# Two-layer encoder, MLP with Strassen block products: four instead of six up chunks ahead, runs of four steps, and shared sums that ScalarE copies out and fills in again

## The chip, the core and the metric

One core of one Trainium2 chip runs the whole network in one launch. The metric is device microseconds, the median of several executions. TensorE is called PE here, VectorE DVE, ScalarE ACT, GpSimd POOL, and SyncE, whose queue issues most loads, SP. PSUM is the memory into which PE's matmuls add; SBUF is the core's other memory.

## The reference

The input is 256 tokens of width 2048. Each of two layers does attention and then a dense MLP:

```python
h = h + jnp.concatenate([mix, cross], axis=-1) @ w_o[i]
n = rms_norm(h, mlp_norm[i])
h = h + jnp.square(jax.nn.relu(n @ w_up[i])) @ w_down[i]
...
return rms_norm(h, final_norm)
```

`w_up` is 2048 x 8192 and `w_down` 8192 x 2048, in float32. The change touches only the MLP: the up product, the squared ReLU, and the down product with its sum into `h`.

## The kernel before

**Precision.** Every float32 operand is split into a high and a low part (`split`, L507 on ACT for the high one, L508 on DVE for the low one), and each product is three matmuls: high by high, high by low, low by high.

**Up chunks.** The 8192 columns of the up product are 64 chunks of 128. A chunk (`up_grains`) loads a megabyte of `w_up` (`raw_U`), splits it in two halves (`uh` on ACT, `ul` on DVE), and runs 48 matmuls 256 wide into `ps_u` (`products`, L411). `squared` then applies ReLU and square on ACT (L1113, L1114). Two chunks make a pair; after the second, DVE forms three more combinations of their four 128 x 128 blocks (`c`, L1122 to L1124), and the seven operands are split into `a_s` (high on ACT, low on DVE). The first `LEAD` = 6 chunks of a layer run by themselves.

**Steps.** The down product is done by Strassen's scheme for 2 x 2 blocks: the 256 tokens are two halves, a pair gives two blocks of the inner dimension, and the 2048 output columns are two halves q, each with two 512-wide blocks. One step (`down_grains`) is one pair and one half q. It loads four 512-wide blocks of `w_down` (`b`), forms combinations of them (`t`: one on ACT, L1165, with an add by a POOL DMA, L1166, and three on DVE, L1172 to L1174), splits them (`bh`, `bl`, and `th`, `tl`), and multiplies seven operand pairs into seven PSUM sums p1 to p7, 512 wide. The products p3, p1, p2 come first (9 matmuls, from `bh`, `bl`), then p7, p6, p4, p5 (12, from `th`, `tl`), each three matmuls at L1194, L1196 and L1197. Between the two groups PE runs one more up chunk, so that 58 steps carry the remaining 58 chunks: the order written out in `add_mlp` is first products, chunk's first half, chunk's second half, second products.

**Runs.** Steps with the same q follow each other in runs (`RUNS`): the seven sums stay in PSUM through a run and leave it at its end (`taken`). p2, p3, p4 belong to one output block each and are added into `h` by DVE (L1237). p1, p5, p6, p7 are shared by several output blocks: the first run of a half q copies them to `z` in SBUF by ACT (L1250), and each later run of that q adds to `z` by DVE (L1248). After the last run of a half, `folded` makes the four output blocks out of `z` by eight DVE instructions (four at L1261, four at L1237), queued with a gap of 3 grains of the plan, 0.5 at the very end.

**Plain chunks.** The inner dimension that the steps leave over (30 pairs are done for one half q, 28 for the other, of 32) is done plainly behind the steps (`plain_grains`), block after block of 512 output columns in the order `REST` = 2, 0, 1, 3: 1 + 1 + 2 + 2 chunks of 24 matmuls 512 wide, with operands `h_p`, `l_p` and `a_p`, into `ps_m` (L388, L391, L392). In layer 0 the finished blocks go into `h` (L1237), are squared for the next norm (L920, ACT), transposed (L626, DVE) and scaled into `nT` (L537 ACT, L538 DVE), the operand of layer 1's first projection, whose weights are split as `uh`/`ul` and `hi`/`lo`. In layer 1 the last block is cut into three pieces, the first token half 512 wide and the second in two of 256, and each is finished by `finish` (add L1405, squares L1415, scaling L1429 to L1431, output DMAs).

**What sets the order.** Each engine runs its instructions in the order of a plan that is written out in grains; loads, splits and copies are placed a set number of grains ahead of their use, `later(k, f)` puts `f` k grains on, and `past(f, x)` behind an instruction x. Each engine's queue is in order: an instruction that waits holds up those behind it.

Of the kernel before, what the change touches and what calls it, by code (L numbers as in the profile page):

```python
# [13 lines left out]
AF = mybir.ActivationFunctionType  # L14
# [21 lines left out]
FIRST_CHUNKS = 3  # L36
UPS = DFF // P

LEAD = 6

RUNS = ((1, 4), (0, 8), (1, 8), (0, 8), (1, 8), (0, 8), (1, 8), (0, 6))

STEPPED = [sum(n for x, n in RUNS if x == q) for q in range(2)]

# [115 lines left out]
def encoder_kernel(ctx: ExitStack, tc: tile.TileContext, t: dict, out: bass.AP):  # L160
# [206 lines left out]
    def later(n, fn, *args):  # L367
        pending.append((state["tick"] + n, fn, args))
# [778 lines left out]
    def down_grains(layer, n, begins, ends, sooner):  # L1147

        q, j = STEPS[n]
        own = {}  # L1150

        def load():
            own["b"] = at.side.tile([P, 4, 512], F32, tag="b", bufs=3, name="b")
            nc.sync.dma_start(own["b"].rearrange("p a b -> p (a b)"),
                              t[f"w_pair{layer}"][j * 2 + q])

        def behind(fn, far=4):

            return (lambda: past(fn, box["splits"][-far])) if n < 2 else fn

        def lift():

            b, s = own["b"], at.side.tile([P, 4, 512], F32, tag="T", bufs=2, name="t")
            own["t"] = s
            nc.scalar.activation(s[:, 3, :], b[:, 3, :], AF.Copy)  # L1165
            nc.gpsimd.dma_start(s[:, 3, :], b[:, 1, :], accum_op=ALU.add)  # L1166

        def pre():

            b, s = own["b"], own["t"]  # L1170
            with tc.issue_after(box["made"].ins) if n == 2 else nullcontext():
                nc.vector.tensor_tensor(s[:, 0, :], b[:, 3, :], b[:, 0, :], op=ALU.add)  # L1172
# [12 lines left out]
        def run(which, products):  # L1185
            if n == 0 and which == "first":
                open_strassen(layer)
            hi, lo = own.pop(which)
            a = box["a", j]
            for name, ai, bi in products:  # L1190
                if begins:
                    sum_of(name)
                ps, s = box["ps"][name], slice(bi * 512, (bi + 1) * 512)
                ins = nc.tensor.matmul(ps, a[:, 0, ai, :], hi[:, s], start=begins, stop=False)  # L1194
                pin(ins)
                nc.tensor.matmul(ps, a[:, 0, ai, :], lo[:, s], start=False, stop=False)  # L1196
                nc.tensor.matmul(ps, a[:, 1, ai, :], hi[:, s], start=False, stop=ends)  # L1197

        def after(products):
            if ends:  # L1200
                for name, _, _ in products:
                    taken(q, name)

        def after_second():
            after(SECOND)
            if ends:
                box["z_set"].add(q)
            if ends and j == STEPPED[q] - 1:
                folded(q, 0.5 if n == len(STEPS) - 1 else 3)

        return [Grain(lambda: run("first", FIRST), lambda: after(FIRST), load, behind(pre), behind(prep_first, 4 if n else 1),
                      (12, 8, 4) if sooner else (12, 5, 4), behind(lift)),
                Grain(lambda: run("second", SECOND), after_second, None, None, behind(prep_second), SOONER)]

    def open_strassen(layer):
# [23 lines left out]
    def taken(q, name):  # L1239

        ps, inv = box["ps"][name], box["inv"]
        if name in DIRECT:
            i, b = DIRECT[name]
            add_scaled(columns_of(i, q, b), ps, inv[:, i : i + 1])
            return
        z = box["z"][q][:, SHARED.index(name), :]
        if q in box["z_set"]:
            nc.vector.tensor_tensor(z, ps, z, op=ALU.add)  # L1248
        else:
            nc.scalar.activation(z, ps, AF.Copy)  # L1250

    DIRECT = {"p2": (1, 0), "p3": (1, 1), "p4": (0, 0)}
    SHARED = ("p1", "p5", "p6", "p7")
# [1 line left out]
    def folded(q, gap):  # L1255

        z1, z5, z6, z7 = (box["z"][q][:, n, :] for n in range(4))
        inv, ninv = box["inv"], box["ninv"]

        def add(d, x, y, op=ALU.add):  # L1260
            return lambda: nc.vector.tensor_tensor(d, x, y, op=op)  # L1261
# [4 lines left out]
        for n, fn in enumerate((out(1, 0, z1, inv), add(z6, z6, z1, ALU.subtract), add(z7, z6, z7, ALU.subtract),  # L1266
                                add(z6, z6, z5, ALU.subtract), out(1, 1, z6, inv), out(0, 0, z7, inv),
                                add(z7, z7, z5, ALU.subtract),
                                out(0, 1, z7, ninv))):
            later(1 + int(gap * n), lambda fn=fn: past(fn, box["splits"][-2]))  # L1270

    def plain_grains(layer, nb, at_chunk):
# [14 lines left out]
                box["rest"] = split(*own[c, hf], own[c][:, hf * HALF : (hf + 1) * HALF])  # L1287


        PIECES = [(c, hf, (2 - nc_ + c) * 4 + hf * 2, 2) for c in range(nc_) for hf in range(2)]  # L1290

        def begin():
            if nb == REST[0]:
# [58 lines left out]
    def down_done(layer, nb):  # L1352
        def f(w):
# [22 lines left out]
            if n < 2:  # L1376
                later(1, turn)
                later(3, come)
            elif n == 2:

                later(2, lambda: past(turn, box["rest"]))
                later(7, lambda: past(come, box["early", 1]))
# [394 lines left out]
```

## Time and profile before

| what | value |
|---|---|
| runs | 1992.29, 1992.8, 1993.76 us; median 1992.8 us |
| span of the profiled execution | 1991.2 us |
| PE busy | 1982.2 us, 100% of the span |
| DVE busy | 1717.2 us, 86% |
| ACT busy | 1330.5 us, 67% |
| POOL busy | 132.8 us, 7% |
| DMA, mean over the span | 225 GB/s |

The profiled execution is known by its span, from its first instruction to its last. Its time as a run isn't listed apart; the median of the runs is 1.6 us above the span, which is what lies around it. In rows of the timeline, the first number is the start in us, the second the duration, and the bracket at the end gives the idle time before and what ended it. In rows of groups, `xN` is the count, then follow busy us in all, mean ns of one, and the idle time before with what ended it. In rows of windows, the columns are the stretch, its length, then busy us of PE, PE's weight loads, DVE, ACT and POOL with their counts, the granted clock of PE, the DMA share and GB/s.

### The profile page before, as it was taken

The page shows a single profiled execution, that of the slowest core. Times are in us where ns is not written, and L with a number is a line of the kernel's source. Part 1 is how long each engine was busy: PE and PEld are TensorE (multiplying, and loading weights), DVE is VectorE, ACT ScalarE, POOL GpSimd, SP SyncE. Part 2 cuts the span into 40 slices and gives each one's busy share as a digit, 9 for nine tenths or more (in the row PEclk, how much of TensorE's full clock was granted, in tenths as well). Part 3 has the DMA queues.
Part 4 walks back from the last instruction along what each step waited for, and adds up shares of the span by engine and source line. Part 5 has one row for each costly group of instructions (what it writes and reads, how often), then busy time and mean ns, then how long its engine had stood idle before and what let it go on. Part 6 is the DMA issues. An engine that isn't in the chain of part 4 may idle for free.

```text
span 1991.2 us, 32845 instructions
## 1 busy us (share of the span) xinstructions
PE 1982.2 (100%) x12856; PEld 1800.9 (90%) x12856; DVE 1717.2 (86%) x2104; ACT 1330.5 (67%) x1861; POOL 132.8 (7%) x185
## 2 busy tenths in 40 slices
PE   9999999999999999999999999999999999999998
PEld 8999999899999999999998888889999999999997
DVE  6777767589899999999999879778998999999997
ACT  6655555577777777777676666667776777777674
POOL 0000000000000000000000011000000000000000
PEclk9999999999999999999999999999999999999999
DMA  7855555767777777777766765667777777777772
GB/s 291 321 194 203 208 187 184 271 194 246 234 229 233 227 225 238 238 236 227 219 217 211 246 216 174 220 194 249 237 224 235 226 227 237 233 238 228 225 237 104
DMA packets 107804, 447.21 MB, mean 225 GB/s; under 512 B 18561, under 2 KB 40321, under 8 KB 60289
## 3 DMA queue, kind: packets, MB, share of 16 engines
q1 hardware_dynamic: 90144, 413.38, 58.9%
q0 software_dynamic: 17216, 31.20, 9.7%
q8 instruction: 101, 1.65, 0.3%
q10 hardware_dynamic: 288, 0.52, 0.1%
q14 instruction: 55, 0.44, 0.1%
HBM read 397.78 MB, written 4.19 MB: 202 GB/s over the span
## 4 chain that ended last, share of the span: by engine, by line
PE 98%; ACT 1%; DVE 1%; issue 0%; DMA 0%; SPq 0%; DVEq 0%; POOL 0%; POOLq 0%; ACTq 0%
PE ps_u L411 35%; PE ps_s L411 9%; PE p L1194 9%; PE p L1197 9%; PE p L1196 9%; PE ps_m L391 8%; PE ps_m L392 8%; PE ps_m L388 8%; PE sc_ps L603 0%; PE sc_ps L605 0%; PE sc_ps L604 0%; PE av L696 0%; PE av L697 0%; PE av L698 0%; PE idle L240 0%
## 5 line engine op out<-in xcount | busy, mean ns | idle before, releaser
L411 PE MATMUL ps_u<-hT,uh 128*128 128x256 f32 x3812 | 663.4, 276 | 0.0
L411 PEld LDWEIGHTS ps_u<-hT,uh 128*128 128x128 f32 x3812 | 578.9, 188 | 5.5
L411 PE MATMUL ps_u<-hT,ul 128*128 128x256 f32 x1960 | 541.4, 276 | 0.0
L507 ACT ACTIVATE uh<-raw_U 128x1024 fp32r<-128x1024 f32 x262 | 276.8, 1057 | 201.5 <-PE ps_u L411 189.3
L411 PEld LDWEIGHTS ps_u<-hT,ul 128*128 128x128 f32 x1960 | 368.0, 188 | 0.0
L508 DVE TENSOR_TENSOR lo<-raw,hi 128x1024 fp32r<-128x1024 f32 (+1 forms) x215 | 255.0, 1190 | 107.8 <-ACT hi L507 106.8
L507 ACT ACTIVATE hi<-raw 128x1024 fp32r<-128x1024 f32 (+1 forms) x215 | 221.9, 1037 | 183.9 <-PE ps_m L392 93.4
L508 DVE TENSOR_TENSOR ul<-raw_U,uh 128x1024 fp32r<-128x1024 f32 x262 | 318.4, 1218 | 13.7 <-ACT uh L507 13.4
L508 DVE TENSOR_TENSOR tl<-t,th 128x2048 fp32r<-128x2048 f32 x116 | 265.5, 2289 | 70.3 <-ACT th L507 69.9
L507 ACT ACTIVATE th<-t 128x2048 fp32r<-128x2048 f32 x116 | 222.7, 1919 | 114.7 <-PE p L1197 114.7
L508 DVE TENSOR_TENSOR bl<-b,bh 128x1536 fp32r<-128x1536 f32 x116 | 203.1, 1751 | 0.0
L1194 PE MATMUL p<-th,a_s 128*128 128x512 f32 x464 | 181.2, 391 | 0.0
L1196 PE MATMUL p<-tl,a_s 128*128 128x512 f32 x464 | 181.0, 390 | 0.0
L1197 PE MATMUL p<-th,a_s 128*128 128x512 f32 x464 | 180.5, 389 | 0.0
L507 ACT ACTIVATE bh<-b 128x1536 fp32r<-128x1536 f32 x116 | 172.4, 1487 | 8.4
L1166 POOL DMA_DIRECT2D t<-b x116 | 100.7, 868 | 1143.5 <-ACT t L1165 1113.2
L411 PE MATMUL ps_s<-nT,hi 128*128 128x256 f32 x896 | 154.6, 277 | 0.0
L1197 PE MATMUL p<-bh,a_s 128*128 128x512 f32 x348 | 136.2, 391 | 0.0
L411 PEld LDWEIGHTS ps_s<-nT,hi 128*128 128x128 f32 x896 | 135.3, 188 | 0.2
L1196 PE MATMUL p<-bl,a_s 128*128 128x512 f32 x348 | 135.4, 389 | 0.0
L1194 PE MATMUL p<-bh,a_s 128*128 128x512 f32 x348 | 135.4, 389 | 0.0
L411 PE MATMUL ps_s<-nT,lo 128*128 128x256 f32 x448 | 124.2, 277 | 0.0
(308 smaller groups left out, 3573.0 us busy)
## 6 DMA issues: line engine op xcount, KB each, us to landing
raw_U<-in_w_up SPq DMA_DIRECT2D x128, 1024.0 KB, 5.7
b<-in_w_pair SPq DMA_DIRECT2D x116, 1024.0 KB, 5.8
raw<-in_w_o SPq DMA_DIRECT2D x32, 1024.0 KB, 4.9
t<-b POOLq DMA_DIRECT2D x116, 256.0 KB, 5.2
raw<-in_w_b SPq DMA_DIRECT2D x21, 1024.0 KB, 5.2
raw<-in_w_av SPq DMA_DIRECT2D x12, 1024.0 KB, 5.0
raw<-in_w_aq SPq DMA_DIRECT2D x12, 1024.0 KB, 4.9
raw<-in_w_ak SPq DMA_DIRECT2D x12, 1024.0 KB, 4.8
```

What stands on the lines that cost most here:

```text
L388: first = nc.tensor.matmul(ps, ah, hi[:, s], start=st, stop=False)
L391: nc.tensor.matmul(ps, ah, lo[:, s], start=False, stop=False)
L392: final = nc.tensor.matmul(ps, al, hi[:, s], start=False, stop=sp)
L411: ins = nc.tensor.matmul(ps, x, acts[:, k, part], start=k == n == 0, stop=k == KT - 1 and n == 2)
L507: first = nc.scalar.activation(dst_hi, src, AF.Copy)
L508: return first, nc.vector.tensor_tensor(dst_lo, src, dst_hi.bitcast(F32), op=ALU.subtract)
L1166: nc.gpsimd.dma_start(s[:, 3, :], b[:, 1, :], accum_op=ALU.add)
L1194: ins = nc.tensor.matmul(ps, a[:, 0, ai, :], hi[:, s], start=begins, stop=False)
L1196: nc.tensor.matmul(ps, a[:, 0, ai, :], lo[:, s], start=False, stop=False)
L1197: nc.tensor.matmul(ps, a[:, 1, ai, :], hi[:, s], start=False, stop=ends)
```

## The change

It sets `LEAD` to 4, so that a layer's steps start after four up chunks and there are 60 steps, 30 for each half q; one plain chunk is left for each of the four blocks, so a layer has 4 instead of 6. `RUNS` becomes sixteen runs: 2, then fourteen of 4, then 2. At the end of every run ACT copies the shared sums to `z`. At the start of the next run of that half, `seeded` has ACT copy `z` back into the PSUM sum, and the run's matmuls add to it; the DVE adds into `z` go. `folded` comes with a gap of 1 instead of 3 and makes one output block earlier; some loads are placed at other distances.

```diff
{DIFF}
```

Counted over the kernel: 84 more matmuls 512 wide in steps, 84 fewer 512 wide and 24 fewer 256 wide in plain chunks. ACT: 112 more copies `z<-p` (128 instead of 16) and 112 copies `p<-z`, four more each of `t`, `bh`, `th` and `u_0`, four fewer each of `h_p` and of the single left block `a_0`. DVE: the 48 adds `z<-p,z` go, the direct adds from p become 96 instead of 48, four more each of `bl`, `tl` and the three `t`, four fewer `l_p`. SP: two loads of `b` more and two plain loads fewer in a layer; POOL: four more DMA adds into `t`. Behind the change the lines of `taken` and later functions are numbered 4 to 6 higher (L1237 is L1241, L1261 is L1267, L1405 is L1411).

The first place is the start of layer 0's steps, on DVE. `tl` is the low part of the first step's second operands, `bl` that of the second step's first operands, `ul` a chunk's low half, `a_s` the low part of the second pair (chunks 2 and 3). Before:

```order
L1124 TENSOR_TENSOR c_4842<-c_4842 128x128
L508 TENSOR_TENSOR bl_4956<-b_4780,bh_4955 128x1536
L508 TENSOR_TENSOR ul_4989<-raw_U_4845,uh_4988 128x1024
L508 TENSOR_TENSOR a_s_4911<-c_4842,a_s_4911 128x896
L508 TENSOR_TENSOR ul_5029<-raw_U_4845,uh_5028 128x1024
L508 TENSOR_TENSOR tl_5070<-t_4811,th_5069 128x2048
```

The second pair's `a_s` stands ahead of the first `tl` (the last row). After the change:

```order
L508 TENSOR_TENSOR tl_4928<-t_4683,th_4927 128x2048
L1122 TENSOR_TENSOR c_4848<-c_4848 128x128
L508 TENSOR_TENSOR bl_4961<-b_4815,bh_4960 128x1536
L1123 TENSOR_TENSOR c_4848<-c_4848 128x256
L926 TENSOR_REDUCE ss_t_5023<-ssq0_130 128x2
L1124 TENSOR_TENSOR c_4848<-c_4848 128x128
L1172 TENSOR_TENSOR t_4957<-b_4922 128x512
L508 TENSOR_TENSOR ul_4991<-raw_U_4851,uh_4990 128x1024
L928 TENSOR_SCALAR full_5025<-ss_t_5023 128x2
L1173 TENSOR_TENSOR t_4957<-t_4957,b_4922 128x512
L508 TENSOR_TENSOR a_s_4919<-c_4848,a_s_4919 128x896
```

Now the first `tl` stands ahead, then `bl`, `ul` and the rest, and the second pair's `a_s` is the eleventh from it.

The second place is ACT where a run of q = 0 ends and one of q = 1 begins. `z0` and `z1` are the two halves' `z`, p7, p6, p5 the shared sums, `th` the high part of the next step's second operands, `c` the ReLU and square. After the change:

```order
L1113 ACTIVATE c_6321<-ps_u_6372 128x256
L1250 ACTIVATE z0_4652<-p7_6022 128x512
L1114 ACTIVATE c_6321<-c_6321 128x256
L1250 ACTIVATE z0_4652<-p6_6025 128x512
L1256 ACTIVATE p7_6454<-z1_4653 128x512
L1256 ACTIVATE p6_6457<-z1_4653 128x512
L1250 ACTIVATE z0_4652<-p5_6030 128x512
L507 ACTIVATE th_6469<-t_6257 128x2048
L1256 ACTIVATE p5_6462<-z1_4653 128x512
L507 ACTIVATE bh_6485<-b_6340 128x1536
```

Before, ACT had no fill anywhere, and `z` copies only at the end of each half's first run; at every other run's end DVE had:

```order
L1248 TENSOR_TENSOR z0_4652<-p7_7273,z0_4652 128x512
L508 TENSOR_TENSOR ul_8004<-raw_U_7859,uh_8003 128x1024
L1248 TENSOR_TENSOR z0_4652<-p6_7277,z0_4652 128x512
L1122 TENSOR_TENSOR c_7891<-c_7891 128x128
L1237 SCALAR_TENSOR_TENSOR first_83<-p4_7281,inv_5023,first_83 128x512
L1174 TENSOR_TENSOR t_7931<-t_7931,b_7910 128x512
L1248 TENSOR_TENSOR z0_4652<-p5_7285,z0_4652 128x512
L508 TENSOR_TENSOR tl_8029<-t_7827,th_8028 128x2048
```

The adds at L1248 have left DVE; ahead of ACT's `th` now stand three copies and two fills, and p5's fill stands behind it.

The third place is the boundary between the layers, on DVE. `ps_m` are sums of plain blocks, `n_t` and `n_z` the transposed blocks, `nT1` the operand of layer 1, `ul` and `lo` the lows of its weights. Before:

```order
L508 TENSOR_TENSOR ul_11416<-raw_U_11298,uh_11415 128x1024
L538 SCALAR_TENSOR_TENSOR nT1_11271<-n_z_11330,first_83,nT1_11271 128x256 x4
L508 TENSOR_TENSOR ul_11432<-raw_U_11298,uh_11431 128x1024
L1237 SCALAR_TENSOR_TENSOR first_83<-ps_m_11391,inv_5023,first_83 128x512
L1237 SCALAR_TENSOR_TENSOR first_83<-ps_m_11392,inv_5023,first_83 128x512
L508 TENSOR_TENSOR lo_11475<-raw_U_11355,hi_11474 128x1024
```

After:

```order
L1241 SCALAR_TENSOR_TENSOR first_83<-ps_m_11548,inv_5027,first_83 128x512
L538 SCALAR_TENSOR_TENSOR nT1_11474<-n_t_11478,first_83,nT1_11474 128x256 x2
L1241 SCALAR_TENSOR_TENSOR first_83<-ps_m_11549,inv_5027,first_83 128x512
L508 TENSOR_TENSOR ul_11565<-raw_U_11450,uh_11564 128x1024
L626 STREAM_TRANSPOSE n_t_11612<-first_83 128x4x4x32
L508 TENSOR_TENSOR ul_11595<-raw_U_11450,uh_11594 128x1024
L626 STREAM_TRANSPOSE n_t_11612<-first_83 128x4x4x32
L538 SCALAR_TENSOR_TENSOR nT1_11474<-n_z_11537,first_83,nT1_11474 128x256 x2
L1241 SCALAR_TENSOR_TENSOR first_83<-ps_m_11598,inv_5027,first_83 128x512
L538 SCALAR_TENSOR_TENSOR nT1_11474<-n_z_11537,first_83,nT1_11474 128x256 x2
L1241 SCALAR_TENSOR_TENSOR first_83<-ps_m_11599,inv_5027,first_83 128x512
L508 TENSOR_TENSOR lo_11648<-raw_U_11505,hi_11647 128x1024
```

Before, layer 1's first `ul` comes behind the transposes of the third block, and the last block's sums behind the second `ul`. After, the third block's sums (the first two L1241 here) stand between the `nT1` of the block before, right ahead of the first `ul`; the transposes of the third block stand around the second `ul`, and the last block's sums between the next four `nT1`, all of it ahead of the first `lo`.

More of the change, by code (lines that the diff above doesn't have):

```diff
@@ L37 @@
 UPS = DFF // P
-LEAD = 6
-RUNS = ((1, 4), (0, 8), (1, 8), (0, 8), (1, 8), (0, 8), (1, 8), (0, 6))
+LEAD = 4
+RUNS = ((1, 2), *((0, 4), (1, 4)) * 7, (0, 2))
 STEPPED = [sum(n for x, n in RUNS if x == q) for q in range(2)]
@@ L1190, in run @@
             for name, ai, bi in products:
-                if begins:
+                if n == 0:
                     sum_of(name)
+                entered = begins and not (name in SHARED and q in box["z_set"])
                 ps, s = box["ps"][name], slice(bi * 512, (bi + 1) * 512)
-                ins = nc.tensor.matmul(ps, a[:, 0, ai, :], hi[:, s], start=begins, stop=False)
+                ins = nc.tensor.matmul(ps, a[:, 0, ai, :], hi[:, s], start=entered, stop=False,
+                                       skip_group_check=True)
                 pin(ins)
-                nc.tensor.matmul(ps, a[:, 0, ai, :], lo[:, s], start=False, stop=False)
-                nc.tensor.matmul(ps, a[:, 1, ai, :], hi[:, s], start=False, stop=ends)
+                nc.tensor.matmul(ps, a[:, 0, ai, :], lo[:, s], start=False, stop=False, skip_group_check=True)
+                nc.tensor.matmul(ps, a[:, 1, ai, :], hi[:, s], start=False, stop=ends, skip_group_check=True)
         def after(products):
@@ L1202, in after @@
                     taken(q, name)
+                    if n + 1 < len(STEPS):
+                        seeded(STEPS[n + 1][0], name)
         def after_second():
@@ L1245, in taken, with seeded @@
             return
[L1246 to L1250, printed above, removed]
+        nc.scalar.activation(box["z"][q][:, SHARED.index(name), :], ps, AF.Copy)
+    def seeded(q, name):
+        ps = sum_of(name)
+        if name in SHARED and q in box["z_set"]:
+            nc.scalar.activation(ps, box["z"][q][:, SHARED.index(name), :], AF.Copy)
     DIRECT = {"p2": (1, 0), "p3": (1, 1), "p4": (0, 0)}
@@ L1266, in folded @@
         for n, fn in enumerate((out(1, 0, z1, inv), add(z6, z6, z1, ALU.subtract), add(z7, z6, z7, ALU.subtract),
-                                add(z6, z6, z5, ALU.subtract), out(1, 1, z6, inv), out(0, 0, z7, inv),
+                                out(0, 0, z7, inv), add(z6, z6, z5, ALU.subtract), out(1, 1, z6, inv),
                                 add(z7, z7, z5, ALU.subtract),
@@ L1381, in f @@
                 later(2, lambda: past(turn, box["rest"]))
-                later(7, lambda: past(come, box["early", 1]))
+                later(5, lambda: past(come, box["early", 1]))
             else:
```

6 lines of the change are left out of this document (3 added, 3 removed).

## The prediction

> **What bounds the kernel now.** I read the head of the page first, then the chain that ended last, then the waits of PE, then windows and timelines of single places.
>
> ```profile
> span 1991.2 us, 32845 instructions
> PE 1982.2 (100%) x12856; PEld 1800.9 (90%) x12856; DVE 1717.2 (86%) x2104; ACT 1330.5 (67%) x1861; POOL 132.8 (7%) x185
> PE 98%; ACT 1%; DVE 1%; issue 0%; DMA 0%; SPq 0%; DVEq 0%; POOL 0%; POOLq 0%; ACTq 0%
> ...
> PE idle L240 <- POOL mhalf L234: 1.0, 1, 1.0
> PE ps_m L391 <- DVE lo L508: 0.2, 1, 0.2
> ```
>
> PE is busy for the whole span, owns 98% of the chain, and waits 1.2 us in all. So the time is PE's work plus the ends; whatever the change does on DVE or ACT shows only where PE must wait for it. The span is 1991.2 us and the median of the runs 1992.8, so 1.6 us lie around the span. I work out a difference against the span and add it to the median. DVE is the engine to watch. Eight steady steps give:
>
> ```profile
> 1577.33:1659.14 81.81, 81.81 (x554) 75.13 (x554) 76.10 (x80) 58.36 (x69) 6.89 (x8) 1.00 0.74 232
> ```
>
> A step takes 81.81/8 = 10.23 us of PE, all of it busy (the second number is PE, then weight loads, DVE, ACT). DVE fills 93% of it and ACT 71%. DVE thus gains only about 0.7 us on PE in a step: once it is behind, it stays behind for steps.
>
> **PE's work.** The layers go from 58 to 60 steps: 4 x 21 = 84 more matmuls 512 wide. Four plain chunks go: 3 x 24 + 12 = 84 matmuls 512 wide fewer, and 24 fewer of 256 in the last block, whose second half is done in two pieces.
>
> ```profile
> 1551.47 0.39 PE L1194 MATMUL p<-bh,a_s 128*128 128x512 f32 x1
> 1551.70 0.39 PE L1196 MATMUL p<-bl,a_s 128*128 128x512 f32 x1
> ...
> 1983.02 0.28 PE L391 MATMUL ps_m<-l_p,a_p 128*128 128x256 f32 x1
> 1983.14 0.28 PE L392 MATMUL ps_m<-h_p,a_p 128*128 128x256 f32 x1
> ```
>
> The wide ones cancel at 0.23 us each. The narrow ones start 0.12 us apart: 24 x 0.12 = **-2.9 us**. The up matmuls are the same in number. That is all the change can gain.
>
> **Sixteen runs instead of eight.** Per layer 16 x 4 sums leave by an ACT copy, and 14 x 4 are seeded by a second one; the 48 DVE adds go, and 48 direct adds come.
>
> ```profile
> L1248 DVE TENSOR_TENSOR z<-p,z 128x512 f32<-128x512 f32 x48 | 32.9, 685 | 0.5 <-PE p L1197 0.5
> L1237 DVE SCALAR_TENSOR_TENSOR first<-p,inv,first 128x512 f32<-128x512 f32 x48 | 35.9, 748 | 4.9 <-PE p L1197 4.9
> L1250 ACT ACTIVATE z<-p 128x512 f32<-128x512 f32 x16 | 9.5, 592 | 0.9 <-PE p L1197 0.9
> L1165 ACT ACTIVATE t<-b 128x512 f32<-128x512 f32 x116 | 72.8, 627 | 20.8 <-DVE tl L508 18.0 <-DMA b<-in_w_pair 1.7 <-DVE u_b L508 1.1
> ```
>
> In eight steps (two transitions against one) DVE goes from 76.1 to 76.1 - 4 x 0.69 + 3 x 0.75 = 75.6. For ACT, the copy out of PSUM costs 0.59; no row shows ACT filling PSUM. The nearest are that copy, 0.59, and SBUF to SBUF of the same size, 0.63. I take 0.62 and keep 0.5 to 1.0 for the range. ACT goes to 58.4 + 8 x 0.59 + 8 x 0.62 = 68.0 of 81.8, so it isn't full. The Trainium skill, "ScalarE: Activation LUTs", under "Step-by-step: what each stage is for", says that ScalarE writes PSUM with less latency than SBUF; by that the fill would be below 0.6, nothing here shows it, and the sum would fall by a few tenths at most.
>
> What counts is the order on ACT at a transition: copies of p7, p6 and two fills stand ahead of the next `th`, and p5's copy too.
>
> ```profile
> 1561.47 0.39 PE L1197 MATMUL p<-th,a_s 128*128 128x512 f32 x1
> 1561.90 1.92 ACT L507 ACTIVATE th<-t 128x2048 fp32r<-128x2048 f32 x1 [1.07 <-PE p L1197]
> 1564.39 0.69 DVE L1248 TENSOR_TENSOR z<-p,z 128x512 f32<-128x512 f32 x1
> 1564.99 2.28 DVE L508 TENSOR_TENSOR tl<-t,th 128x2048 fp32r<-128x2048 f32 x1
> ...
> 1569.43 0.39 PE L1196 MATMUL p<-tl,a_s 128*128 128x512 f32 x1
> ```
>
> (On DVE and ACT the next instruction starts some 0.08 before the end that a row gives, as 1564.39 + 0.69 against 1564.99; I count start to start.) `th` starts when the last th matmul has ended, and `tl` is wanted 7.5 us later. After the change ACT has, from p7's end (2.05 us before the last matmul's end), three copies, two fills and about 0.7 of small work: 1.5 + 1.1 + 0.7 = 3.3, so `th` starts 1.3 us late. Then 1.96 + 2.2 to the end of `tl`: 5.5 of the 7.5 us. **No stall, 2 us to spare**; at 0.05 more per fill it is 0.1 less. Cover gone, every 0.1 us beyond costs 28 x 0.1 = 2.8 us. In the steady steps I therefore take 0.
>
> **Four chunks ahead instead of six.** Pair 1 (chunks 2 and 3) is wanted by step 1.
>
> ```profile
> 449.70 1.08 DVE L508 TENSOR_TENSOR a_s<-c,a_s 128x896 fp32r<-128x896 f32 x1
> 451.77 0.40 PE L1194 MATMUL p<-bh,a_s 128*128 128x512 f32 x1
> 454.19 2.29 DVE L508 TENSOR_TENSOR tl<-t,th 128x2048 fp32r<-128x2048 f32 x1 [2.28 <-ACT th L507]
> ```
>
> Before, its low half `a_s` is done at 450.8, a whole step before its use, and ahead of the first `tl`. After, it stands behind that `tl` (the rows above). With T the end of chunk 3, PE wants it at T + 9 x 0.23 (first products) + 48 x 0.1135 (a chunk) + 12 x 0.23 + 2 x 0.23 = T + 10.7. In the rows T is 451.77 and `tl` starts at T + 2.4; now one `uh` stands ahead on ACT, about 0.9: T + 3.3. DVE then has, by these rows and those above:
>
> ```profile
> L508 DVE TENSOR_TENSOR tl<-t,th 128x2048 fp32r<-128x2048 f32 x116 | 265.5, 2289 | 70.3 <-ACT th L507 69.9
> L508 DVE TENSOR_TENSOR bl<-b,bh 128x1536 fp32r<-128x1536 f32 x116 | 203.1, 1751 | 0.0
> L508 DVE TENSOR_TENSOR ul<-raw_U,uh 128x1024 fp32r<-128x1024 f32 x262 | 318.4, 1218 | 13.7 <-ACT uh L507 13.4
> L1172 DVE TENSOR_TENSOR t<-b 128x512 f32<-128x512 f32 x116 | 79.3, 684 | 0.0
> L508 DVE TENSOR_TENSOR a_s<-c,a_s 128x896 fp32r<-128x896 f32 x60 | 65.1, 1084 | 2.2 <-ACT a_s L507 2.2
> ```
>
> tl 2.2, bl 1.67, ul 1.13, two t 1.2, small ones 0.9, a_s 1.08: 8.2, so T + 11.5. PE waits 0.8 plus the signal, 0.9, in each layer: **+1.8**.
>
> **Two plain chunks fewer behind the steps.** In layer 0 that takes 48 x 0.2275 = 10.9 us of PE from the stretch in which DVE clears its queue. Before:
>
> ```profile
> 1043.35 0.69 DVE L1248 TENSOR_TENSOR z<-p,z 128x512 f32<-128x512 f32 x1 [0.26 <-PE p L1197]
> ...
> 1073.97 1.20 DVE L508 TENSOR_TENSOR ul<-raw_U,uh 128x1024 fp32r<-128x1024 f32 x1
> 1078.05 0.39 PE L391 MATMUL ps_m<-ul,nT 128*128 128x512 f32 x1
> ...
> L1261 DVE TENSOR_TENSOR z<-z 128x512 f32<-128x512 f32 x16 | 10.9, 684 | 0.1
> L626 DVE STREAM_TRANSPOSE n_t<-first 128x512 f32<-128x512 f32 x6 | 6.3, 1086 | 0.0
> L538 DVE SCALAR_TENSOR_TENSOR nT<-xT,first,nT 128x256 fp32r<-128x256 f32 x16 | 6.7, 474 | 0.0
> ```
>
> DVE waited for PE at 1043.35, so it was abreast; from there it worked without a gap and had layer 1's first `ul` at 1075.2, 2.9 us ahead of PE. After: let S be the start of the last second products. DVE last waits ahead of the `tl` of step 58, at S - 17.7 (end of step 57) + 1.6 (the transition on ACT) + 2.0 = S - 14.1. Until the first `ul` of layer 1 it has 2 `tl` 4.4, `bl` 1.7, 11 `ul` or `l_p` 12.4, 16 adds into h at 0.66 (10.6), 6 folds of z at 0.6 (3.6), `a_p` 0.6, 4 transposes 4.1, 4 `nT` 1.6, and 0.4 for signals: 39.4 us, so S + 25.3. PE wants it after 12 + 96 + 1 matmuls, S + 24.8. With the signal PE waits 0.8. Next, `hi` stands on ACT behind the square of a sum that DVE adds only after a transpose, `ul`, a transpose and two `nT`: S + 25.3 + 1.0 + 1.13 + 1.0 + 0.8 + 0.75 = S + 30.0, then square 0.7, `hi` 1.06 and signals: S + 32.0. PE is there 23 matmuls after its first wait, S + 30.8: another 1.2. `lo` follows 1.2 later, with signal 1.1 beyond the one matmul that PE can do: **+3.1** in all.
>
> **The tail.** The last block's pieces are now 12 matmuls each: PE ends 2.9 us after the first piece, before 5.8.
>
> ```profile
> 1977.71 0.75 DVE L1405 SCALAR_TENSOR_TENSOR first<-ps_m,inv,first 128x512 f32<-128x512 f32 x1 [1.79 <-PE ps_m L392]
> ...
> 1981.50 0.48 DVE L1405 SCALAR_TENSOR_TENSOR first<-ps_m,inv,first 128x256 f32<-128x256 f32 x1
> ...
> 1983.46 0.48 DVE L1405 SCALAR_TENSOR_TENSOR first<-ps_m,inv,first 128x256 f32<-128x256 f32 x1 [0.41 <-PE ps_m L392]
> ```
>
> The first piece's finish takes DVE from 1977.71 to 1981.9 and was hidden; the third piece started right at PE's end. After, DVE comes to the first piece 0.9 late (same lag as at the boundary), and the third piece stands 4.0 behind it: 4.9 against PE's 2.9. **+2.0**, 1.0 of it even with no lag.
>
> **Sum:** -2.9 + 1.8 + 3.1 + 2.0 = +4.0; span 1995.2, time **1996.8**. SP's loads move by a step at most and POOL's adds stay ahead of their use: 0.
>
> **Rivals.** *DVE keeps up* (not slower): if `th` of step 58 starts 0.8 us earlier, the lag at S is gone; the boundary costs 2.3, the tail 1.2, sum +2.4, 1995.2. For it: the fill may be short; against: ACT's order. 0.20. With no wait anywhere the time is 1992.8 - 2.9 = 1989.9; 0.08, and speaking against it is that the tail's chain alone gives back 1.0. *ACT or DVE binds at transitions*: fill at 1.0 us, or other engines slowed while all three work on PSUM, uses the 2 us; 0.2 us beyond gives 28 x 0.2 = 5.6, 2002. 0.14. *PE's clock falls in a stall*:
>
> ```profile
> 1985.00:1986.00 1.00, 0.00 (x0) 0.00 (x0) 0.86 (x2) 0.72 (x1) 0.11 (x1) 1.00 0.00 0
> 1986.00:1987.00 1.00, 0.00 (x0) 0.00 (x0) 0.42 (x1) 0.00 (x0) 0.00 (x0) 0.59 0.11 37
> ```
>
> The granted clock (the number before DMA share) fell some 2.6 us after the last matmul. The boundary's waits add up to 3.1, but lie in pieces of 1.4 or less; in one piece, with PE at half speed for 3 us after, they cost 1.5 more: 1998.3. 0.04. The Trainium skill, "TensorE: Matmul & The Clock Gate", Part 1, has the clock halved after an idle window of about 3.4 us and freed after as much busy time; by that no wait here is long enough, and one that was would cost 1.7. *The change doesn't do what it says*: the rows above show that it does; none.
>
> **Chances and range.** My forecast 0.54, in which longer waits are likelier than shorter: 1% on 39 us of DVE work is 0.4 at the boundary and again in the tail. A measurement tells 0.2%, 4.0 us: 1988.8 and 1996.8. The forecast lies on that bound: 0.36 of it slower, 0.18 same. Slower: 0.36 + 0.14 + 0.04 = 0.54. Same: 0.18 + 0.20 + 0.05 = 0.43. Faster: the last 0.03 of the case with no wait, since even that saves only 2.9. The range goes from 1993.5 (half the waits) to 2001.0 (transitions 0.15 us short): the ends leave out about 0.15.
>
> **What would show it.** PE's waits should list `a_s` in both layers at 0.9, and `ul`, `hi`, `lo` once each at the boundary; no wait at L1194 to L1197 in the steady steps; fills of 0.6; the third piece some 2 us behind PE's end. A wait for `tl` or a sum at every transition would make the steady step's term wrong; a third piece right at PE's end, the tail's.

## The result and the profile after

The changed kernel takes 1999.59 us, median of five (1998.24 to 2000.67), against 1993.06 us before (1992.29 to 1993.76): a ratio of 1.0031, with a 95% interval of 1.002 to 1.0043. It is slower by 0.31%. The forecast was 1996.8 us, slower, with a range from 1993.5 to 2001.0.

The profiled execution is the shortest of the five, 1998.24 us; its span is 5.3 us longer than that of before, where the medians lie 6.5 apart. The head of the page and its chain:

```profile
span 1996.5 us, 33058 instructions
PE 1981.3 (99%) x12832; PEld 1797.1 (90%) x12832; DVE 1735.5 (87%) x2112; ACT 1432.0 (72%) x2089; POOL 136.6 (7%) x189
PE 93%; DVE 3%; DMA 2%; ACT 1%; issue 0%; SPq 0%; DVEq 0%; POOLq 0%; POOL 0%; ACTq 0%
```

PE runs 24 matmuls fewer, and the span is longer all the same. The chain of work that ended last, 98% PE before, now goes 3% over DVE and 2% over DMA. The waits of PE (engine, line, who was waited for; us in all, times, the longest):

```profile
PE p L1199 <- DVE a_s L508: 1.6, 3, 0.6
PE ps_m L388 <- ACT hi L507: 1.0, 1, 1.0
PE idle L240 <- POOL mhalf L234: 1.0, 1, 1.0
PE ps_m L391 <- DVE ul L508: 0.6, 1, 0.6
PE ps_m L391 <- DVE lo L508: 0.5, 1, 0.5
PE ps_m L392 <- DVE nT L538: 0.4, 1, 0.4
...
PE p L1195 <- ACT a_s L507: 0.2, 1, 0.2
```

`a_s`, `hi`, `ul`, `lo` are the four names that the prediction gave. None of them lies in the steady steps. A wait in this view is the idle time alone; a matmul behind a wait also starts later after it, so I count start to start, beyond the 0.23 us of a running stream.

The table cuts the span at matmuls of the timeline: first up matmul of a layer, first product of its steps, first plain matmul, first projection of layer 1, last matmul, end. Two experiments stand beside it.

| stretch, us | before | after | after - before | PE's work alone | lead6b | start1 |
|---|---|---|---|---|---|---|
| to the first up chunk | 418.17 | 418.23 | 0.06 | 0 | 418.38 | 418.72 |
| layer 0: ups and steps | 627.01 | 638.42 | 11.41 | 9.56 | 627.01 | 637.19 |
| layer 0: plain chunks | 32.64 | 21.76 | -10.88 | -10.92 | 32.64 | 21.76 |
| layer 1's attention | 245.47 | 249.17 | 3.70 | 0 | 245.43 | 249.93 |
| layer 1: ups and steps | 627.01 | 637.45 | 10.44 | 9.56 | 627.01 | 636.59 |
| layer 1: plain chunks | 33.11 | 22.07 | -11.04 | -11.07 | 33.11 | 22.07 |
| last matmul to the end | 7.78 | 9.36 | 1.58 | 0 | 7.77 | 9.37 |

PE's work is -2.9 in all (42 matmuls of 0.2275 more in a layer's steps, the plain ones fewer). The rest, +8.1, lies at the three places: 1.85 + 0.88 at the starts of the steps, 3.7 at the boundary, 1.6 in the tail.

**The steps.** Eight of them, with two transitions between runs (windows; columns as before the change):

```profile
586.23:668.04 81.81, 81.81 (x553) 75.15 (x552) 76.14 (x79) 65.15 (x85) 6.98 (x8) 1.00 0.75 232
```

It is the same 81.81 us as before, all PE. DVE has 76.1 us, as before, and ACT rose from 58.4 to 65.2; the forecast was 75.6 and 68.0. The groups of ACT that copy sums out, fill them in, and copy within SBUF:

```profile
L1250 ACT ACTIVATE z<-p 128x512 f32<-128x512 f32 x128 | 76.1, 595 | 1.0 <-PE p L1199 1.0
L1165 ACT ACTIVATE t<-b 128x512 f32<-128x512 f32 x120 | 75.0, 625 | 6.9 <-DMA b<-in_w_pair 5.9 <-DVE tl L508 0.9
L1256 ACT ACTIVATE p<-z 128x512 f32<-128x512 f32 x112 | 65.8, 610 | 0.0
```

A fill is 0.61 us, beside the 0.62 that was taken. The chain at a transition, in the timeline: the last matmul that reads the old `th`, then `th`, `tl`, and PE's first use of `tl`.

```profile
586.00 0.39 PE L1199 MATMUL p<-th,a_s 128*128 128x512 f32 x1
...
587.59 1.93 ACT L507 ACTIVATE th<-t 128x2048 fp32r<-128x2048 f32 x1
589.55 2.29 DVE L508 TENSOR_TENSOR tl<-t,th 128x2048 fp32r<-128x2048 f32 x1 [0.96 <-ACT th L507]
...
593.96 0.39 PE L1198 MATMUL p<-tl,a_s 128*128 128x512 f32 x1
```

`th` starts 1.2 us later than in a plain step (587.59 - 586.00 against 561.90 - 561.47), and `tl` ends at 591.84, 2.1 us ahead of its use.

**The start of layer 0's steps**, in the chain of work that ended last (start, us, what), and behind it PE's waits:

```profile
426.30 9.56 DMA b<-in_w_pair
...
435.88 0.69 DVE t L1172
...
440.02 0.30 DVE c L1124
...
440.35 0.95 ACT a_s L507
```

```profile
441.35 0.50 PE L1195 MATMUL p<-bh,a_s 128*128 128x512 f32 x1 [0.18 <-ACT a_s L507]
...
442.48 0.50 PE L1199 MATMUL p<-bh,a_s 128*128 128x512 f32 x1 [0.39 <-DVE a_s L508]
453.60 0.50 PE L1199 MATMUL p<-bh,a_s 128*128 128x512 f32 x1 [0.59 <-DVE a_s L508]
```

The last wait is the one forecast, on pair 1. The other two are on the high and the low half of pair 0 and were not forecast: the load of `b` for the second step took 9.56 us, DVE stood before its first combination until 435.88, and the combinations of pair 0 (`c`) stand behind it.

**The boundary**, DVE and PE:

```profile
1040.05 2.29 DVE L508 TENSOR_TENSOR tl<-t,th 128x2048 fp32r<-128x2048 f32 x1
...
1078.42 1.24 DVE L508 TENSOR_TENSOR ul<-raw_U,uh 128x1024 fp32r<-128x1024 f32 x1
```

```profile
1079.71 0.50 PE L391 MATMUL ps_m<-ul,nT 128*128 128x512 f32 x1 [0.64 <-DVE ul L508]
...
1086.01 0.73 PE L388 MATMUL ps_m<-hi,nT 128*128 128x512 f32 x2 [1.00 <-ACT hi L507]
1087.27 0.50 PE L391 MATMUL ps_m<-lo,nT 128*128 128x512 f32 x1 [0.53 <-DVE lo L508]
...
1094.53 0.51 PE L392 MATMUL ps_m<-uh,nT 128*128 128x512 f32 x1 [0.40 <-DVE nT L538]
```

With S = 1053.93, `tl` starts at S - 13.9 and `ul` ends at S + 25.7; the forecast had S - 14.1 and S + 25.3. Start to start PE loses 0.84, 1.16 and 0.69, and 0.57 more on `nT` behind the last block's transposes; behind each of the four, one more matmul comes 0.1 late.

**The tail**, the pieces on DVE, and windows of one us (the last three numbers are granted clock, DMA share, GB/s):

```profile
1984.88 1.31 DVE L1411 SCALAR_TENSOR_TENSOR first<-ps_m,inv,first 128x512 f32<-128x512 f32 x2
...
1988.75 0.48 DVE L1411 SCALAR_TENSOR_TENSOR first<-ps_m,inv,first 128x256 f32<-128x256 f32 x1
```

```profile
1989.00:1990.00 1.00, 0.00 (x0) 0.00 (x0) 0.72 (x3) 0.00 (x0) 0.17 (x1) 1.00 0.60 225
...
1991.00:1992.00 1.00, 0.00 (x0) 0.00 (x0) 0.70 (x1) 0.14 (x1) 0.00 (x0) 0.57 1.02 397
...
1994.00:1995.00 1.00, 0.00 (x0) 0.00 (x0) 0.00 (x0) 0.00 (x0) 0.00 (x0) 0.50 0.76 297
```

(The first row holds the first two pieces.) The third piece starts 1.64 us behind PE's end at 1987.11; before, it started 0.04 behind it. From its start to the end of the span it is 7.72 us, before 7.74, so the late third piece is the whole 1.6. Beside it the DMA engines are full from 1989.4 to 1994.8: the two megabytes of output now leave one right behind the other.

### The profile page after: what moved, and what is told of

Same layout as the page of the kernel before. It is cut to its first block, busy times and chain, and to the rows that moved or that the text cites. A ratio compares the mean times of both kernels' runs of the same rounds, so it can differ in the third digit from the quotient of the medians.

```text
span 1996.5 us, 33058 instructions
## 1 busy us (share of the span) xinstructions
PE 1981.3 (99%) x12832; PEld 1797.1 (90%) x12832; DVE 1735.5 (87%) x2112; ACT 1432.0 (72%) x2089; POOL 136.6 (7%) x189
## 3 DMA queue, kind: packets, MB, share of 16 engines
q8 instruction: 100, 1.64, 0.3%
## 4 chain that ended last, share of the span: by engine, by line
PE 93%; DVE 3%; DMA 2%; ACT 1%; issue 0%; SPq 0%; DVEq 0%; POOLq 0%; POOL 0%; ACTq 0%
PE ps_u L411 33%; PE ps_s L411 10%; PE p L1199 9%; PE p L1195 9%; PE p L1198 9%; PE ps_m L392 7%; PE ps_m L391 7%; PE ps_m L388 7%; DMA b<-in_w_pair 1%; DMA n_t<-n_t 0%; DVE ul L508 0%; DVE bl L508 0%; SPq L629 0%; DVE nT L538 0%; ACT uh L507 0%
## 5 line engine op out<-in xcount | busy, mean ns | idle before, releaser
L411 PE MATMUL ps_u<-hT,uh 128*128 128x256 f32 x3874 | 674.0, 277 | 0.0
L411 PEld LDWEIGHTS ps_u<-hT,uh 128*128 128x128 f32 x3874 | 588.6, 188 | 5.7
L411 PE MATMUL ps_u<-hT,ul 128*128 128x256 f32 x1994 | 551.3, 277 | 0.0
L411 PEld LDWEIGHTS ps_u<-hT,ul 128*128 128x128 f32 x1994 | 374.6, 188 | 0.0
L508 DVE TENSOR_TENSOR tl<-t,th 128x2048 fp32r<-128x2048 f32 x120 | 274.8, 2290 | 52.8 <-ACT th L507 52.5
L507 ACT ACTIVATE th<-t 128x2048 fp32r<-128x2048 f32 x120 | 230.8, 1923 | 91.7 <-PE p L1199 91.7
L508 DVE TENSOR_TENSOR bl<-b,bh 128x1536 fp32r<-128x1536 f32 x120 | 210.2, 1752 | 0.0
L1195 PE MATMUL p<-th,a_s 128*128 128x512 f32 x480 | 187.6, 391 | 0.0
L1198 PE MATMUL p<-tl,a_s 128*128 128x512 f32 x480 | 187.4, 390 | 0.0
L1199 PE MATMUL p<-th,a_s 128*128 128x512 f32 x480 | 186.9, 389 | 0.0
L1199 PE MATMUL p<-bh,a_s 128*128 128x512 f32 x360 | 141.5, 393 | 1.6 <-DVE a_s L508 1.6
L1195 PE MATMUL p<-bh,a_s 128*128 128x512 f32 x360 | 140.3, 390 | 0.2 <-ACT a_s L507 0.2
```

Of the source, the lines that this page charges most:

```text
L411: ins = nc.tensor.matmul(ps, x, acts[:, k, part], start=k == n == 0, stop=k == KT - 1 and n == 2)
L507: first = nc.scalar.activation(dst_hi, src, AF.Copy)
L508: return first, nc.vector.tensor_tensor(dst_lo, src, dst_hi.bitcast(F32), op=ALU.subtract)
L1195: ins = nc.tensor.matmul(ps, a[:, 0, ai, :], hi[:, s], start=entered, stop=False, skip_group_check=True)
```

## The experiments

Times are medians; each ratio is to before, with its 95% interval, before at 1992.96 to 1993.08 in the same runs. "The changed kernel" is 1999.59. In some of the kernels the lines are numbered one or two higher than in the changed one.

### Do runs of four and ScalarE's copies cost anything?

**lead6.** Six chunks ahead again, runs of four kept:

```diff
-LEAD = 4
+LEAD = 6
-RUNS = ((1, 2), *((0, 4), (1, 4)) * 7, (0, 2))
+RUNS = ((1, 2), *((0, 4), (1, 4)) * 7)
```

> Six chunks ahead again, 58 steps in runs of four (one of two at the start), six plain chunks a layer; shared sums stay with ScalarE's copies and fills. Theory (PE's waits lie at the start of the steps, at the layer boundary and in the tail, none in the steps): PE's work is that of before, the waits for a_s go, the boundary has its 10.9 us of cover back; only a rest in the tail, up to 1.5 us. Time 1993 to 1995, some 5 us below the changed kernel. Rival (copies and fills at the run transitions cost time in the steps): the transitions are all still there, so at least 1997.

1996.61 us, 1.0018 (1.0009 to 1.0026): between the two. The steps are those of before to the digit, 593.41 us in each layer, but the boundary keeps 1.7 us and the tail 1.4. This kernel differs from before in one thing more: its last run belongs to q = 1, so q = 0 has two pairs fewer, and the two plain chunks fall to the two middle blocks. (Before, in the order 2, 0, 1, 3 the chunks are 2, 1, 1 and 2, since q = 1 has 28 steps; the description of the kernel ahead of the prediction gives 1, 1, 2, 2, which is wrong.) So the last block has one chunk, as in the changed kernel.

**lead6b.** The same with the halves exchanged:

```diff
-RUNS = ((1, 2), *((0, 4), (1, 4)) * 7)
+RUNS = ((0, 2), *((1, 4), (0, 4)) * 7)
-                later(5, lambda: past(come, box["early", 1]))
+                later(7, lambda: past(come, box["early", 1]))
```

> As the kernel with six chunks ahead and runs of four, but the halves change places (first run of two for q = 0, last run for q = 0, as before the change), so the six plain chunks fall to the blocks in before's order, two for the first and two for the last, and not two for each of the middle blocks. Theory (runs of four with ScalarE's copies and fills cost nothing; what is left is plain chunks behind the steps and in the last block): boundary and tail are those of before, 1993 within 1 us. Rival (VectorE enters the end later with runs of four, whatever the plain chunks): the boundary's 1.7 us and the tail's 1.4 stay, 1996.

1993.14 us, 1.0001 (0.9991 to 1.001): before's time, and every stretch of the table is before's within 0.2 us. Its waits of PE:

```profile
PE idle L240 <- POOL mhalf L234: 1.0, 1, 1.0
PE ps_s L411 <- ACT hi L507: 0.4, 1, 0.4
PE ps_s L411 <- DVE lo L508: 0.2, 1, 0.2
```

None is in the MLP (`ps_s` are the projections of the attention). Fifteen runs with all their copies and fills cost nothing, and the rival, transitions that cost, falls. The tail goes with the plain chunks of the last block. At the boundary two things changed from lead6 to lead6b, the order of the plain chunks and the place of `come`, which scales the third block into `nT`; these two runs don't tell them apart.

**seed2 and seed3.** Every fill two (shown) or three times:

```diff
+            for _ in range(2):
-            nc.scalar.activation(ps, box["z"][q][:, SHARED.index(name), :], AF.Copy)
+                nc.scalar.activation(ps, box["z"][q][:, SHARED.index(name), :], AF.Copy)
```

> The changed kernel with every fill of a PSUM sum issued twice by ScalarE (the same data, so 112 copies more, 0.53 us each). Theory: two fills stand ahead of the next th at a transition, th starts 1.06 us later, and of the 2 us to spare 1 is left: the same time as the changed kernel within 1 us. Rival (ScalarE binds at the transitions already): 28 x 1.06 = 30 us more.

> The changed kernel with every fill issued three times by ScalarE. Theory: th now starts 2.1 us later than with one fill, the 2 us to spare are used up, so the steps begin to lose time at the 28 transitions: between 1 and 80 us more than the changed kernel, with PE waiting for tl or th in the second products behind a transition. Rival (ScalarE has far more room than the count from the rows says): no change, below 2001.

seed2: 1999.56 us, 1.0034 (1.0022 to 1.0047), the changed kernel's time. seed3: 2093.76 us, 1.0509 (1.0493 to 1.0525), 94 us more. Both expectations named the wrong place: the second fills of p7 and p6 stand behind `th`, not ahead of it, so `th` isn't delayed; of the 2.1 us ahead of `tl` these runs say nothing. What they show is ScalarE's room elsewhere. seed2, a transition in ACT's timeline (the second fills are among the three behind `th`):

```profile
589.99 1.93 ACT L507 ACTIVATE th<-t 128x2048 fp32r<-128x2048 f32 x1
591.80 1.65 ACT L1257 ACTIVATE p<-z 128x512 f32<-128x512 f32 x3
```

seed3, PE's waits, the first row:

```profile
PE p L1195 <- ACT p L1257: 54.6, 49, 1.9
```

With four fills more at a transition ACT still makes it; with eight, the last one ends after PE wants the sum, and PE waits up to 1.9 us for it, at nearly every transition. These waits are 55 of the 94 us. Part of the rest is PE's clock: the granted clock fell to 0.50 for 3.41 us thirteen times in seed3's span, twelve of them within a microsecond behind one of the 26 waits of 1.9 us, and at half the clock 3.41 us lose at most 1.7.

**dvesums.** Shared sums added on DVE as before the change, no fills, all else as changed:

```diff
-                entered = begins and not (name in SHARED and q in box["z_set"])
+                entered = begins
...
-        nc.scalar.activation(box["z"][q][:, SHARED.index(name), :], ps, AF.Copy)
+        z = box["z"][q][:, SHARED.index(name), :]
+        if q in box["z_set"]:
+            nc.vector.tensor_tensor(z, ps, z, op=ALU.add)
+        else:
+            nc.scalar.activation(z, ps, AF.Copy)
...
-        if name in SHARED and q in box["z_set"]:
+        if False:
```

> The changed kernel, but shared sums are added to z by VectorE as before the change (112 adds at 0.60 us start to start), and nothing is filled in. Theory: in eight steps VectorE has 76.1 + 4 x 0.60 + 3 x 0.75 = 80.8 of 81.8 us, so it can't make up for a delay; it enters the ends of both layers several us late: 10 to 15 us above the changed kernel, with the waits at the boundary and the tail, none spread evenly over the steps. Rival (ScalarE's copies and fills are what costs): faster than the changed kernel by 2 us or more.

2016.76 us, 1.0118 (1.0104 to 1.0131): 17 us above the changed kernel, somewhat more than expected. The largest waits:

```profile
PE p L1199 <- DVE a_s L508: 7.1, 9, 0.9
PE ps_m L388 <- DVE first L1241: 3.3, 2, 1.6
```

The second row is at the ends, as expected. The first was not: six of those waits lie within the steps, most of them 165 us apart. With the sums added on DVE, runs of four cost 17 us; with ScalarE's copies they are free.

### The start of the steps

**astart2** holds the third step's `t` back behind pair 1's low `a_s`; **start1** also holds the second step's behind pair 0's:

```diff
-            split(a[:, 0], a[:, 1], c[:, 1:])
+            box["made"] = split(a[:, 0], a[:, 1], c[:, 1:])[1]
```

```diff
-            with tc.issue_after(box["made"].ins) if n == 2 else nullcontext():
+            with tc.issue_after(box["of", n - 1].ins) if n in (1, 2) else nullcontext():
```

The first diff is astart2's; start1 also keeps that instruction as `box["of", pair]`.

> The changed kernel with the third step's first combination t held back behind the low a_s of the second pair, so that a_s is done about 1.2 us earlier at the start of the steps. Theory: the waits for that a_s, 0.75 us in each layer, go: 1.5 us less than the changed kernel, 1998.1. Rival (the waits come from the late load of b and move on to the next operand): no change.

> The changed kernel with the combinations t of the second step held back behind the first pair's low a_s, and those of the third step behind the second pair's. Theory (the first pair's a_s is late in layer 0 because VectorE stands ahead of it in a wait for the second step's load of b): the waits for a_s go in both steps, 0.56 + 0.75 + 0.75 in the profile, 2 us or somewhat more less than the changed kernel, and about 0.5 less than with the second pair's alone: 1997. Rival (ScalarE, which waits for the same load ahead of the squares, holds the pair back as much): no better than 1997.5.

astart2: 1997.52 us, 1.0024 (1.0015 to 1.0033), 2.1 less than the changed kernel. start1: 1996.69 us, 1.0018 (1.0009 to 1.0027), 2.9 less. In astart2's profile the two late starts on pair 1 (0.75 us each) are gone and the one on pair 0's low half (0.56) is left; in start1's that is gone too. Its waits of PE begin with the boundary's, and none of them names `a_s`:

```profile
PE ps_m L388 <- ACT hi L507: 1.0, 1, 1.0
...
PE ps_m L391 <- DVE ul L508: 0.6, 1, 0.6
PE ps_m L391 <- DVE lo L508: 0.5, 1, 0.5
```

Its layer 1 comes to 636.59 us, which is before's 627.01 and the 9.56 of PE's work. So the order on DVE makes the waits on both pairs; in layer 0, DVE's wait for the load of `b` in front of pair 0's `c` makes those on pair 0.

start1's attention of layer 1 takes 249.93 us, 0.8 more than in the changed kernel, though the waits `ul`, `hi` and `lo` are the same. Its windows behind them:

```profile
1087.00:1088.00 1.00, 1.00 (x5) 0.80 (x4) 0.69 (x2) 0.00 (x0) 0.00 (x0) 0.72 1.12 225
1088.00:1089.00 1.00, 1.00 (x4) 0.73 (x3) 0.00 (x0) 0.98 (x2) 0.00 (x0) 0.50 0.82 273
...
1090.00:1091.00 1.00, 1.00 (x4) 0.78 (x4) 1.00 (x2) 1.00 (x4) 0.00 (x0) 0.57 1.02 426
```

The granted clock (the third number from the end) is 0.50 from 1087.45 to 1090.86, and eight matmuls in a row start about 0.43 apart instead of 0.23. That costs 1.6 us; in return the wait on `nT` is gone. The profiles of astart2, both and poolfold show the same fall of 3.41 us at this place, those of the changed kernel, seed2, tailact and fix don't, with waits there that are as long. What decides it these runs don't show.

### The boundary

**nofold** leaves out the subtractions on `z` (`return lambda: None` in the same place, so the blocks made from `z` lack them; it is run for its time only), **poolfold** gives them to GpSimd:

```diff
-            return lambda: nc.vector.tensor_tensor(d, x, y, op=op)
+            return lambda: nc.gpsimd.tensor_tensor(d, x, y, op=op)
```

> The changed kernel without the four subtractions on z at each half's end, so the output blocks made from z are left wrong; its time alone counts. Theory (VectorE's queue without a gap sets the boundary's waits and the lag in the tail): six of the 0.60 us instructions go from that stretch, 3.6 us, so the waits at the boundary, 3.3 us in the profile, fall below 0.7 and the tail gains up to 0.9: 3 to 4 us less than the changed kernel. Rival (the boundary waits for the transposing DMAs or for ScalarE's order): less than 1 us gained.

> The changed kernel with the four subtractions on z at each half's end on GpSimd instead of VectorE. Theory (VectorE's queue sets the boundary's waits): as with the subtractions left out, 3 to 4 us less than the changed kernel, 1996. Rival (GpSimd is slower, and h gets its blocks too late for the next norm or the queue behind them): no gain or a loss.

nofold: 1996.09 us, 1.0027 (1.0001 to 1.0053), 3.5 less than the changed kernel, as the theory has it. The attention of layer 1 takes 246.19 us, 0.7 more than before instead of 3.7; of the waits at the boundary, 0.3 us on a `lo` and 0.2 on an `ul` are left.

The tail gained only 0.16 (9.20 against 9.36). With the lag gone, DVE takes the first piece at once, and the third still stands 4.3 us behind it, against 2.9 of PE.

poolfold: 2003.74 us, 1.0055 (1.0042 to 1.0067), 4.2 more: the rival's loss, though not by waits. The subtractions on GpSimd, and what DVE does beside them:

```profile
L1267 POOL TENSOR_TENSOR z<-z 128x512 f32<-128x512 f32 x16 | 32.1, 2007 | 32.2 <-ACT z L1250 29.0 <-DVE first L1241 2.5
...
1036.30 5.32 POOL L1267 TENSOR_TENSOR z<-z 128x512 f32<-128x512 f32 x3 [2.68 <-ACT z L1250]
1038.66 1.79 DVE L508 TENSOR_TENSOR a_p<-c,a_p 128x512 fp32r<-128x512 f32 x1
1042.24 3.27 POOL L1267 TENSOR_TENSOR z<-z 128x512 f32<-128x512 f32 x1 [0.62 <-DVE first L1241]
1044.29 2.84 DVE L508 TENSOR_TENSOR bl<-b,bh 128x1536 fp32r<-128x1536 f32 x1
```

They take 2.0 us each against 0.68 on DVE. The trace lists no wait of DVE for them. But DVE's own instructions beside them last longer: 1.79 us for an `a_p` that takes 0.69 in the changed kernel, 2.84 for a `bl` of 1.75. Sixteen of them are 0.4 to 1.1 us longer, 14.7 us in all, where the sixteen subtractions would have taken 9.6 of DVE's queue (0.60 each, start to start). So DVE's queue became longer, not shorter, and the loss agrees with the theory that this queue sets the boundary.

### The tail, and the parts together

**tailact** scales 1024 columns of the first token half on ACT; **both** is start1 with this; **fix** is astart2, poolfold and this:

```diff
-        nc.vector.tensor_scalar(h[:, i, 512:x], h[:, i, 512:x], r, None, op0=ALU.mult)
+        if i == 0:
+            nc.scalar.activation(h[:, i, 512:x], h[:, i, 512:x], AF.Copy, scale=r)
+        else:
+            nc.vector.tensor_scalar(h[:, i, 512:x], h[:, i, 512:x], r, None, op0=ALU.mult)
```

> The changed kernel, and in the last block the scaling of 1024 columns of the first token half on ScalarE instead of VectorE. Theory (the third piece waits for VectorE's chain behind the first piece): the third piece starts 0.66 earlier, 0.6 less than the changed kernel, 1999.0. Rival (the output's DMAs set the end): no change.

> The edits at the start of the steps and in the tail together. Theory: they add, 2.0 + 0.6 less than the changed kernel, 1996.5 to 1997, still above before, since the boundary's 3.3 us and most of the tail stay. Rival: the tail's gain is lost to the output's DMAs, 1997.5.

> Both together, and in the last block the scaling of 1024 columns of the first token half on ScalarE instead of VectorE (0.66 us from between the first and the third piece). Theory: boundary down by 2.9, starts by 1.5, tail by 0.7 to 1.0: 1994.3, and since the start in layer 0 still waits for b's load and the tail for its output, not below 1993. Rival: the parts don't add, 1996 or more.

tailact: 2000.1 us, 1.0033 (1.0021 to 1.0046), no gain. Its third piece starts at 1988.02, 3.2 us behind the first instead of 3.9, and the end comes at the same distance from the last matmul, 9.33 us against 9.36. The windows of its tail:

```profile
1989.00:1990.00 1.00, 0.00 (x0) 0.00 (x0) 0.33 (x3) 0.33 (x2) 0.55 (x1) 1.00 0.65 248
1990.00:1991.00 1.00, 0.00 (x0) 0.00 (x0) 0.98 (x2) 0.42 (x1) 0.00 (x0) 0.61 1.05 399
...
1994.00:1995.00 1.00, 0.00 (x0) 0.00 (x0) 0.00 (x0) 0.00 (x0) 0.00 (x0) 0.50 0.66 261
```

From its third piece to the end it is 8.34 us instead of 7.72. The DMA engines fill the same 5.3 us. Before, the first megabyte left between 1982 and 1985, in part beside the last piece's matmuls, and the second from 1987 on; now both leave behind them, and a third piece quicker than the changed kernel's only joins the queue. both: 1997.01 us, 1.002 (1.0011 to 1.0029), start1's time and nothing for the tail. fix: 2001.49 us, 1.0042 (1.003 to 1.0055): GpSimd's loss outweighs the rest. No version here beats the kernel before.

## Why the prediction was right, point by point

- **PE's work, -2.9.** Right: -2.9 by the stretches of the table, and start1's layer 1 has exactly that work.
- **Transitions, 0.** Right, with 2.1 us to spare where 2 were forecast, `th` 1.2 us late where 1.3 were, and 0.61 for a fill where 0.62 was. The Trainium skill, "ScalarE: Activation LUTs", under "Step-by-step: what each stage is for", has PSUM as the lower-latency target of ScalarE's writes, beside SBUF: here a copy takes 0.610 into PSUM and 0.625 into SBUF, both read from SBUF, so it agrees, by 0.015 us. It is not below 0.6, as the prediction took from it. lead6b shows that nothing else there costs.
- **Start of the steps, +1.8.** Too small: 2.7 us in the profile, and edits that take the waits away give back 2.1 (pair 1 alone) and 2.9 us (both pairs) between medians. The term for pair 1 was right in mechanism and nearly in size, 0.75 in each layer. The step that failed is "SP's loads move by a step at most: 0". The load of `b` for the second step was issued when it had been before, at 426.3 (426.2 before), and took as long, 9.6 us (9.4). But it is now wanted ten us sooner, and it stops DVE in front of pair 0's `c`.
- **Boundary, +3.1.** Right in mechanism, 3.7 measured: the three waits come to 2.7, and 0.57 came on a fourth, `nT`, that was not counted. nofold shows that DVE's unbroken queue is the cause. The size of the first wait, 0.84 for 0.8, is partly luck: the forecast's own times, S + 24.8 and S + 25.3, are 0.5 apart, and the rest was put on the signal; in the trace `ul` ends 0.4 later than forecast, and PE starts 0.05 behind it.
- **Tail, +2.0.** Right in mechanism, 1.6 measured: the third piece starts 1.64 us behind PE's end instead of 0.04, and what follows it takes as long as before. Two sizes are off. The lag at the first piece is 0.6 and not 0.9: it starts 2.23 us ahead of PE's end, and 2.83 in nofold, where DVE is there in time. And "1.0 of it even with no lag" is too little: in nofold the third piece still starts 1.46 behind PE's end, so the lag was worth 0.2. What the forecast left out are the output's DMAs. They stand level with the chain of the third piece, so that a shorter chain alone gains nothing, as tailact shows.
- **The sum, +4.0.** 5.3 from profile to profile and 6.5 between medians. The forecast's terms were too small at the start by 0.9 and at the boundary by 0.6, and too large in the tail by 0.4. The other 1.2 us is mostly what the profiled execution lies below its kernel's median, 1.35 us (its span is 1996.5, the five spans go from there to 1998.9); where the others lose it no profile of this kernel shows, and that stays open. A candidate is layer 0's chunks ahead of the steps: in profiles of kernels with four chunks ahead they take 23.1 to 24.7 us, and the changed kernel's profile has the 23.1. In seed2's, which has the 24.7, the load of `b` took 10.6 us instead of 9.6, and PE waited 1.2 us for pair 0's high half instead of 0.2. With six ahead the stretch was 33.60 in three of three.
- **The rival on PE's clock** did not come in this profile: the granted clock is 1.00 until the last matmul is over. But its condition was put too strictly. The prediction asked for the boundary's waits in one piece and took no wait here to be long enough, by the rule that it cites. The measurement decides otherwise: start1, astart2, both and poolfold have the fall behind waits in pieces of 0.5 to 1.6 us, and seed3 behind single ones of 1.9. Its price of 1.5 us is near the 1.6 of start1. It doesn't explain the 1.2 us left open above, at least not in general: a fall of 3.41 us to half takes 0.001 off the mean granted clock, and that is 0.999 in four of the changed kernel's five executions, the profiled one among them, and 0.998 in the fifth (1999.4 us).

## What to carry to other kernels

Moving shared work to an engine with room is free in the steady state if the order on that engine leaves slack on the chain that the bound engine waits for; count it at the transition, in us ahead of the use. What such a change lets you trim elsewhere, here lead-in and tail work of the bound engine, is at the same time the cover for everything that the other engines, the loads and the output do at the ends: price that cover first. At a kernel's end, look at when the output's DMAs start before shortening the arithmetic in front of the last one. And work that is moved to a second engine can slow the first one beside it: compare the durations of the instructions that stay.

## What the runs showed of the hardware

- ScalarE fills PSUM from SBUF in 0.610 us for 128x512 floats, reads it out in 0.595, and copies SBUF to SBUF in 0.625.
- A float subtraction of 128x512 takes 2.01 us on GpSimd in poolfold and 0.68 on VectorE in the changed kernel. VectorE's instructions beside those on GpSimd took up to 1.1 us longer (`a_p` 1.79 instead of 0.69, `bl` 2.84 instead of 1.75).
- PE's granted clock fell to 0.50 for 3.41 us behind waits far shorter than that: 1.0 and 0.5 us within 3 us in start1, 1.9 us in one piece in seed3. It doesn't always: the changed kernel has start1's waits without the fall, and in seed3 twelve of 26 such waits were followed by one.
- PE's granted clock fell 2.8 us after the last matmul in one profile (1983.4 to 1986.2, from 0.59 granted in that us) and 4.0 us after it in another (1987.1 to 1991.1), so the delay isn't fixed.
- A load of 1 MB that lands in 5.8 us as a rule (the median of the loads of `b`) took 9.6 where it followed two others at once, and was what a start then waited for. In before the same load took 9.4 and nothing waited.
